# Head copies by engines to the other 64 partitions, and rotations whose partner rows are added by an accumulating DMA

## The chip, the cores and the metric

The kernel runs on one core of one Trainium2 chip. The metric is the device time of one execution in microseconds (us); lower is better. A core has a matrix engine (TensorE, PE in the profile), a vector engine (VectorE, DVE), a scalar engine (ScalarE, ACT), a general engine (GpSimd, POOL) and a sync engine (SyncE, SP). Each runs its own instructions strictly in the order in which they were written, and waits for the others through semaphores. SP and POOL also issue DMA transfers: those of SP go to the queue "hardware_dynamic" of the profile, those of POOL to "software_dynamic", and the same 16 DMA engines work on both.

## The reference

Two layers run over 528 rows (16 learned tokens and 512 inputs) of width 1024. Each layer makes one large projection and splits it into a convolution group and an attention group:

```python
proj = jnp.einsum('bld,de->ble', h, w_in[l])
a, g, zc, q, k, v, za, qi, ki, wi = jnp.split(proj, IN_SPLITS, axis=-1)
y_conv = conformer_conv_branch(a, g, zc, ...)      # GLU, 31-tap causal conv, LayerNorm, SiLU, gate
q = apply_rope(q.reshape(B, Lp, N_HEADS, HEAD_DIM), cos_h, sin_h)
k = apply_rope(k.reshape(B, Lp, N_HEADS, HEAD_DIM), cos_h, sin_h)
qi = apply_rope(qi.reshape(B, Lp, N_IDX_HEADS, IDX_DIM), cos_h, sin_h)
ki = apply_rope(ki, cos, sin)
y_attn = dsa_sparse_attention(q, k, v, qi, ki, wi, topk) * jax.nn.silu(za)
h = layer_norm(DEEPNORM_ALPHA * h + concat(y_conv, y_attn) @ w_out[l], ...)
```

`apply_rope` turns pairs of channels: `x1*cos - x2*sin` and `x2*cos + x1*sin`. The sparse attention first scores all keys with the indexer heads `qi`, `ki`, keeps the 132 best per query, and attends to these alone. There are 8 attention heads and 8 indexer heads of 64 channels.

## The kernel before

Everything is held transposed: channels lie on the 128 partitions and positions along the free axis. A row tile is 128 x 528 and so holds two heads of 64 channels. Columns of a weight are loaded in halves of 128 x 512 (256 KB): SP loads the half into `wraw` (7 buffers), ACT copies it to `whi` (4 buffers, the rounded high part), ACT writes its negative to `wlo` (5 buffers), and POOL issues a DMA that adds `wraw` to `wlo`, so that `wlo` is the low part. A product is then three runs of matmuls, high by high (`hh`, `whi`), low by high (`hl`, `whi`) and high by low (`hh`, `wlo`).

The work is cut into named jobs: `i0`-`i3` make the indexer queries, `kw` the indexer key and its weights, `s12` and `s34` the scores and top-k on DVE, `q`, `k`, `v`, `a` the parts of a pair of heads, `t0`-`t3` the attention of a pair, `u`, `z`, `c01`, `c23`, `cl` the convolution group, `o0`-`o7` and `oa` the output projection, `ln` the closing norm. `ORDER` gives the order in which jobs are recorded. A planner then schedules all recorded operations with a cost for each (`_price`), a delay from each operation to the ones that depend on it (`delay`), and a shift in time for each job (`SHIFT`), and writes the instructions of each engine in the order that it found. All operations are recorded in one place, so nearly every instruction of a trace has the same line, and the tiles tell them apart.

The functions that matter here are three. `rope` rotates a row tile `x`: rows are stored so that partners lie on neighbouring partitions, two DMAs on SP copy odd rows to even rows and back into `rot`, and DVE makes `x*cos`, `rot*sin` and their sum. `heads_q` splits a rotated tile into high and low parts and lays them out so that one tile holds, for one head, the high part in its own 64 partitions and the low part in the other 64: two copies on ACT, a subtraction on DVE into `lq`, and two DMAs on SP to the other partitions. `heads_k` makes tiles that hold a head's high part (`k0`, `k1`) or its low part (`kl`, `km`) in both halves: three copies on ACT, one subtraction on DVE, and four DMAs on SP. `job_kw` copies the indexer key to both halves of `ki` by two DMAs. Per layer there are eight calls of `heads_q` (four of jobs `i`, four of `q`), four of `heads_k`, and thirteen of `rope`.

Of the kernel before, what the change touches and what calls it, by code (L numbers as in the profile page):

```python
# [8 lines left out]
F32 = mybir.dt.float32  # L9
F32R = mybir.dt.float32r  # L10
BF = mybir.dt.bfloat16
AF = mybir.ActivationFunctionType
OP = mybir.AluOpType
# [6 lines left out]
L = SEQ + NM  # L20
DEPTH = 2
NH = 8
HD = 64
# [10 lines left out]
C_KW = 32  # L34
# [10 lines left out]
)  # L45
SHIFT = {
# [21 lines left out]
}  # L68
W1 = NM + P
K_COS = 0  # L70
K_SIN = L
# [13 lines left out]
class Planner:  # L85
# [84 lines left out]

    def delay(self, a, b, true):
        if a.dma:
            far = 650.0 if a.eng == "pool" else 1950.0
            return far + a.tail + (900.0 if b.eng == "sp" else 1067.0 if b.eng == "pe" else 950.0)
        if a.eng == b.eng and (not true or a.eng == "pe"):
            return 0.0
        return self.LAT.get((a.eng, b.eng), 120) + (200.0 if (a.eng, b.eng, a.tail) == ("dve", "act", 1)
                                                    else 0.0)
# [161 lines left out]
def tile_hymba(ctx: ExitStack, tc: tile.TileContext, xt: bass.AP, wi: bass.AP, wv: bass.AP,  # L340
# [3 lines left out]
    pe, act, dve, pool, sync = (pl.engine(e) for e in ("pe", "act", "dve", "pool", "sp"))  # L344
# [28 lines left out]
    def weight(src, eng, kt=KT, into=None, step=KT // 2):  # L373
        W = [], []
        for k in range(0, kt, step):
            r = T(wp, [P, KT // 2, P], F32, name="wraw", tag="wraw", bufs=7)[:, :step, :]
            sync.dma_start(r, src[:, k:k + step, :])
            if into:
                h, o = [t[:, k:k + step, :] if len(t.shape) == 3 else t for t in into]
                if len(h.shape) == 4:  # L380
                    r = r.rearrange("p (r c) n -> p r c n", r=2)
            else:
                h, o = [T(wp, [P, KT // 2, P], F32R, name=n, tag=n, bufs=b)[:, :step, :]
                        for n, b in (("whi", 4), ("wlo", 5))]
            act.activation(h, r, AF.Copy)
            if eng is pool:
                act.activation(o, r, AF.Copy, scale=-1.0)
                pool.dma_start(o.bitcast(F32), r, accum_op=OP.add)
            else:
                eng.tensor_tensor(o, r, h.bitcast(F32), op=OP.subtract)  # L390
            for w, t in zip(W, (h, o)):
                w.extend(t[:, n, :] if len(t.shape) == 3 else t[:, n // 2, n % 2, :] for n in range(step))
        return W
# [22 lines left out]
    cosT = konst[:, K_COS:K_COS + L]  # L416
    sinT = konst[:, K_SIN:K_SIN + L]
# [25 lines left out]
    for l in range(DEPTH):  # L443
# [4 lines left out]
        def spans(lo):  # L448
            return [(lo, L)] if L - lo <= 512 else [(max(a, lo), b) for a, b in HALVES]

        def project(col, lo, evac):
            w = weight(wi[l, col], *(fresh.pop(0)() if fresh else (pool,)))
            for a, b in spans(lo):
                acc = T(ps, [P, 512], F32, name="acc", tag="acc", bufs=3)[:, :b - a]
                product(acc, w, lambda k: HI[:, k, a:b], lambda k: LO[:, k, a:b])
                evac(acc, a, b)

        def row(name, dt=F32):
            tag, n = {"xq": ("x", 2), "xk": ("x", 2), "ki": ("x", 2), "vt": ("x", 2), "rot": ("rot", 2),
                      "lq": ("lq", 2), "sg": ("sg", 1)}.get(name, ("rl", ROWS))  # L460
            return T(sp, [P, L], dt, name=name, tag=tag, bufs=n)

        def copy_to(x, scale=1.0):
            return lambda acc, a, b: act.activation(x[:, a:b], acc, AF.Copy, scale=scale)

        def rope(x, a):
            rot = row("rot")
            for g in range(2):
                sync.dma_start(rot[g::2, a:], x[1 - g::2, a:])
            dve.tensor_mul(x[:, a:], x[:, a:], cosT[:, a:])  # L470
            dve.tensor_mul(rot[:, a:], rot[:, a:], sinT[:, a:])
            dve.tensor_add(x[:, a:], x[:, a:], rot[:, a:])

        def split(x, a, hi, lo):
            act.activation(hi[:, a:], x[:, a:], AF.Copy)
            dve.tensor_tensor(lo[:, a:], x[:, a:], hi[:, a:].bitcast(F32), op=OP.subtract)

        def heads_q(col, a, keep, scale=1.0):
            x = row("xq")
            project(col, a, copy_to(x, scale))  # L480
            rope(x, a)
            s0, s1 = keep("s0"), keep("s1")
            lo = row("lq", F32R)
            split(x, a, s0, lo)
            act.activation(s1[64:, a:], x[64:, a:], AF.Copy)
            sync.dma_start(s1[:64, a:].bitcast(F32), lo[64:, a:].bitcast(F32))
            sync.dma_start(s0[64:, a:].bitcast(F32), lo[:64, a:].bitcast(F32))
            return s0, s1

        def heads_k(col, keep):  # L490
            x = row("xk")
            project(col, 0, copy_to(x))
            rope(x, 0)
            s0, s1, l0, l1 = (keep(n) for n in ("k0", "k1", "kl", "km"))
            split(x, 0, s0, l0)
            act.activation(s1[64:, :], x[64:, :], AF.Copy)
            act.activation(l1[64:, :], l0[64:, :], AF.Copy)
            for one, two in ((s0, s1), (l0, l1)):
                sync.dma_start(two[:64, :].bitcast(F32), two[64:, :].bitcast(F32))
                sync.dma_start(one[64:, :].bitcast(F32), one[:64, :].bitcast(F32))  # L500
            return (s0, s1), (l0, l1)

        def dots(qs, ks, kls, q0, m, a, b):
            out = [T(ps, [P, 512], F32, name="pl", tag="s", bufs=2)[:m, :b - a] for _ in range(2)]
# [7 lines left out]
        kw = T(sp, [P, L], F32, name="kw", tag="s01")  # L512
# [6 lines left out]

        def job_kw():  # L520
            ki = row("ki")
            project(C_KW, 0, copy_to(kw))
            for s in (0, 64):
                sync.dma_start(ki[s:s + 64, :], kw[0:64, :])
            rope(ki, 0)
            split(ki, 0, kih, kil)
            po = turn(ki, P)
            act.activation(kihr, po, AF.Copy)
            dve.tensor_tensor(kilr, po, kihr.bitcast(F32), op=OP.subtract)
# [188 lines left out]
        def keep(j):  # L718
            return lambda name: T(sp, [P, L], F32R, name=name, tag=f"{name}{j % 2}")

        def job_q(j):
            ready[j, "q"] = (heads_q(C_Q + j, qlo, keep(j), -HD ** -0.5),)
# [135 lines left out]
        for i in range(2):  # L858
            pl.job = f"ln{i}/{l}"
            a, b, _ = chunks(i)  # L860
            norm(lambda j: R[j // 4][:, j % 4, :], KT, mean_c[:, 0, :], i, V_PG, pool, i == 1)
            for j in range(KT):
# [4 lines left out]
                else:  # L867
# [6 lines left out]
                    if not last and j % 2:  # L874
                        pool.tensor_tensor(LO[:, j, a:b], r, HI[:, j, a:b].bitcast(F32),
                                           op=OP.subtract)
# [68 lines left out]
```

## Time and profile before

| | us |
|---|---|
| Median of 3 runs | 675.14 (672.87 to 675.35) |
| The profiled execution | 671.79 |
| Its span, first to last instruction | 669.8 |
| PE busy / DVE busy | 639.0 / 524.0 |
| ACT busy / POOL busy | 463.8 / 191.9 |
| Mean granted TensorE clock | 0.989 of full speed |

Matmuls are pipelined, so PE counts as busy from the start of one to the modelled end of the next, and a busy PE may still be spaced more widely than it could be. A wait in the profile is the idle time just before an instruction, put down to the semaphore that came last.

### The profile page before, as it was taken

Reading aid. Unit: us, or ns where it says so; the run is one execution under the profiler, and the core shown is the slowest. Engines: PE = TensorE matmul, PEld = TensorE weight load, DVE = VectorE, ACT = ScalarE, POOL = GpSimd, SP = SyncE. Lnnn points to the kernel's source line nnn. Section 1 sums busy time; section 2 is a strip of 40 time slices with the busy share of each in tenths; the row PEclk is TensorE's granted clock in tenths of the full one; section 3 lists DMA queues with packets and bytes.
Section 4 is the critical chain, followed back from the end, with each engine's and each line's share of the span. In section 5 each row is a group of like instructions: output and inputs, shape, how many; then the busy total and the mean of one; then the engine's idle time right before and its main releaser. Section 6 shows DMA issues by size and latency. Waiting matters only on the chain.

```text
span 669.8 us, 13204 instructions
## 1 busy us (share of the span) xinstructions
PE 639.0 (95%) x4602; PEld 598.1 (89%) x4602; DVE 524.0 (78%) x1279; ACT 463.8 (69%) x1056; POOL 191.9 (29%) x236
## 2 busy tenths in 40 slices
PE   8999999999999998899999999999999999989993
PEld 7989999999999987899898999888999889967992
DVE  5686999999899947444563999999999999483356
ACT  7554865865756979596676665667549887895536
POOL 0423213223211322444543232223231121233262
PEclk8999999999999999899999999999999999999997
DMA  8899849748855586998315985887886783279503
GB/s 299 203 263 219 237 95 236 168 98 197 198 131 130 127 224 170 200 212 199 75 68 139 225 212 131 191 212 173 189 186 163 166 188 90 87 177 238 82 1 125
DMA packets 67570, 112.60 MB, mean 168 GB/s; under 512 B 7600, under 2 KB 21168, under 8 KB 67376
## 3 DMA queue, kind: packets, MB, share of 16 engines
q0 software_dynamic: 25088, 41.95, 37.5%
q1 hardware_dynamic: 42416, 69.81, 33.2%
q8 instruction: 36, 0.59, 0.3%
q14 instruction: 30, 0.25, 0.1%
HBM read 50.46 MB, written 4.26 MB: 82 GB/s over the span
## 4 chain that ended last, share of the span: by engine, by line
PE 56%; issue 15%; DMA 9%; DVE 6%; ACT 5%; POOL 2%; SPq 0%; POOLq 0%; ACTq 0%; DVEq 0%
PE acc L297 28%; PE acco L297 11%; DMA wlo<-wraw 5%; PE o L297 5%; PE pl L297 3%; PE pp L297 3%; PE pq L297 2%; POOL wlo L297 2%; DVE r L297 2%; DVE sc L297 1%; DMA s<-lq 1%; PE pm L297 1%; DMA kl<-kl 1%; DMA qi<-lq 1%; DMA rot<-xq 1%
## 5 line engine op out<-in xcount | busy, mean ns | idle before, releaser
L297 POOL DMA_DIRECT2D wlo<-wraw x140 | 124.0, 939 | 350.7 <-ACT wlo L297 214.1
L297 DVE SCALAR_TENSOR_TENSOR conv<-u,vec,conv 128x528 f32<-128x528 f32 (+1 forms) x240 | 176.4, 755 | 1.8
L297 PE MATMUL acc<-hh,whi 128*128 128x272 f32 (+3 forms) x872 | 154.0, 308 | 5.0 <-ACT hh L297 2.5
L297 PE MATMUL acc<-hl,whi 128*128 128x272 f32 (+3 forms) x872 | 148.1, 303 | 0.0
L297 PE MATMUL acc<-hh,wlo 128*128 128x272 f32 (+3 forms) x872 | 144.5, 304 | 3.8 <-DMA wlo<-wraw 3.5
L297 PEld LDWEIGHTS acc<-hh,whi 128*128 128x128 f32 x872 | 125.1, 190 | 11.7 <-ACT hh L297 3.9
L297 PEld LDWEIGHTS acc<-hh,wlo 128*128 128x128 f32 x872 | 123.8, 190 | 10.7 <-DMA wlo<-wraw 6.2
L297 ACT ACTIVATE whi<-wraw 128x512 fp32r<-128x512 f32 (+1 forms) x148 | 86.9, 614 | 66.3 <-PE acc L297 51.1
L297 PEld LDWEIGHTS acc<-hl,whi 128*128 128x128 f32 x872 | 124.6, 190 | 3.9 <-issue 0.2
L297 ACT ACTIVATE wlo<-wraw 128x512 fp32r<-128x512 f32 x140 | 85.5, 623 | 6.9 <-PE acc L297 4.8
L297 DVE SCALAR_TENSOR_TENSOR r<-r,acco 128x256 f32<-128x256 f32 (+2 forms) x56 | 25.8, 462 | 47.4 <-PE acco L297 47.3
L297 DVE MAX8 m<-sc 128x8 f32<-128x400 f32 (+3 forms) x106 | 55.9, 551 | 0.0
L297 DVE MATCH_REPLACE8 sc<-m,sc 128x400 f32<-128x400 f32 (+3 forms) x98 | 53.6, 549 | 0.0
L297 ACT ACTIVATE p<-p,ast 128x400 f32<-128x400 f32 (+4 forms) x72 | 40.6, 568 | 5.0 <-DVE ast L297 4.7
L297 PE MATMUL o<-v,pt 128*128 128x64 f32 x320 | 43.0, 265 | 0.5 <-ACT pt L297 0.4
L297 PEld LDWEIGHTS o<-v,pt 128*128 128x128 f32 x320 | 41.5, 192 | 1.7 <-ACT pt L297 1.1
L297 ACT ACTIVATE rl<-pl 128x272 f32<-128x272 f32 (+3 forms) x80 | 29.5, 391 | 14.8 <-PE pl L297 12.1
L297 DVE CUSTOM_DVE_ANT_0 p<-pl,bmask 128x272 f32<-128x272 f32 (+3 forms) x80 | 33.0, 433 | 7.7 <-PE pl L297 6.2
L297 ACT ACTIVATE pt<-pp 128x128 f32<-128x128 f32 (+3 forms) x64 | 26.9, 433 | 11.5 <-PE pp L297 10.7
L297 ACT ACT_TABLE_LOAD x26 | 33.4, 1283 | 1.5 <-PEq L936 0.7
L297 DVE SCALAR_TENSOR_TENSOR sc<-rl,ws,sc 12x144 f32<-12x144 f32 (+3 forms) x56 | 29.9, 555 | 0.6 <-ACT rl L297 0.3
L297 PE MATMUL pp<-konst,p 128*128 128x128 f32 x160 | 30.2, 289 | 0.0
(167 smaller groups left out, 1067.5 us busy)
## 6 DMA issues: line engine op xcount, KB each, us to landing
wlo<-wraw POOLq DMA_DIRECT2D x140, 256.0 KB, 4.9
wraw<-wi SPq DMA_DIRECT2D x128, 256.0 KB, 3.8
wraw<-wo SPq DMA_DIRECT2D x32, 256.0 KB, 4.1
hl<-wraw POOLq DMA_DIRECT2D x16, 256.0 KB, 5.2
rot<-xk SPq DMA_DIRECT2D x16, 132.0 KB, 2.7
k<-k SPq DMA_DIRECT2D x16, 132.0 KB, 3.1
r<-xt SPq DMA_DIRECT2D x2, 1056.0 KB, 8.9
r<-spill SPq DMA_DIRECT2D x2, 1024.0 KB, 6.2
```

Of the source, the lines that this page charges most:

```text
L297: self.plan.record(self.e, fn, lambda: real(*a, **k), reads, writes, *_price(self.e, fn, named, reads, writes))
```

## The change

In `rope` the products come first: `rot = x*sin` with the signs of the table turned round, then `x = x*cos`, and then two DMAs issued by POOL add the rows of `rot` to their partner rows of `x` in flight. The DVE addition is gone, and so are the two DMAs on SP. In `heads_q` the subtraction writes straight to the other 64 partitions, as two instructions of 64 partitions each, and the two DMAs on SP are gone. In `heads_k` six copies on ACT and two subtractions on DVE fill both halves, without the four DMAs. `job_kw` fills `ki` from the accumulator by two more copies on ACT for each part of the row. The planner's delay behind a DMA of POOL is 1800 ns in place of 650 ns, and `SHIFT` has other numbers throughout; `ORDER` is as it was.

```diff
 SHIFT = {
-    "a0/1": 301146, "a1/0": -624491, "a1/1": -132089, "a2/0": 1188874, "a2/1": -413625,
+    "a0/0": 128058, "a0/1": -2790, "a1/0": -360296, "a1/1": -41383, "a2/0": -466571,
...
-            far = 650.0 if a.eng == "pool" else 1950.0
+            far = 1800.0 if a.eng == "pool" else 1950.0
...
         def rope(x, a):
             rot = row("rot")
-            for g in range(2):
-                sync.dma_start(rot[g::2, a:], x[1 - g::2, a:])
+            dve.tensor_mul(rot[:, a:], x[:, a:], sinT[:, a:])
             dve.tensor_mul(x[:, a:], x[:, a:], cosT[:, a:])
-            dve.tensor_mul(rot[:, a:], rot[:, a:], sinT[:, a:])
-            dve.tensor_add(x[:, a:], x[:, a:], rot[:, a:])
+            for g in range(2):
+                pool.dma_start(x[g::2, a:], rot[1 - g::2, a:], accum_op=OP.add)
...
-            s0, s1 = keep("s0"), keep("s1")
-            lo = row("lq", F32R)
-            split(x, a, s0, lo)
-            act.activation(s1[64:, a:], x[64:, a:], AF.Copy)
-            sync.dma_start(s1[:64, a:].bitcast(F32), lo[64:, a:].bitcast(F32))
-            sync.dma_start(s0[64:, a:].bitcast(F32), lo[:64, a:].bitcast(F32))
-            return s0, s1
+            ss = keep("s0"), keep("s1")
+            for g, t in enumerate(ss):
+                own, other = x[64 * g:64 * g + 64, a:], slice(64 - 64 * g, 128 - 64 * g)
+                hi = t[64 * g:64 * g + 64, a:]
+                act.activation(hi, own, AF.Copy)
+                dve.tensor_tensor(t[other, a:], own, hi.bitcast(F32), op=OP.subtract)
+            return ss
...
-            s0, s1, l0, l1 = (keep(n) for n in ("k0", "k1", "kl", "km"))
-            split(x, 0, s0, l0)
-            act.activation(s1[64:, :], x[64:, :], AF.Copy)
-            act.activation(l1[64:, :], l0[64:, :], AF.Copy)
-            for one, two in ((s0, s1), (l0, l1)):
-                sync.dma_start(two[:64, :].bitcast(F32), two[64:, :].bitcast(F32))
-                sync.dma_start(one[64:, :].bitcast(F32), one[:64, :].bitcast(F32))
-            return (s0, s1), (l0, l1)
+            hs, ls = [[keep(n) for n in ns] for ns in (("k0", "k1"), ("kl", "km"))]
+            for g, (h, t) in enumerate(zip(hs, ls)):
+                own, other = slice(64 * g, 64 * g + 64), slice(64 - 64 * g, 128 - 64 * g)
+                act.activation(h[own, :], x[own, :], AF.Copy)
+                dve.tensor_tensor(t[own, :], x[own, :], h[own, :].bitcast(F32), op=OP.subtract)
+                act.activation(h[other, :], x[own, :], AF.Copy)
+                act.activation(t[other, :], t[own, :].bitcast(F32), AF.Copy)
+            return hs, ls
...
-            project(C_KW, 0, copy_to(kw))
-            for s in (0, 64):
-                sync.dma_start(ki[s:s + 64, :], kw[0:64, :])
+
+            def evac(acc, a, b):
+                act.activation(kw[:, a:b], acc, AF.Copy)
+                for g in (0, 64):
+                    act.activation(ki[g:g + 64, a:b], acc[:64], AF.Copy)
+            project(C_KW, 0, evac)
...
-    cst[:, K_SIN:K_SIN + L] = np.tile(np.stack([-sn, sn], axis=1).reshape(HD, L), (2, 1))
+    cst[:, K_SIN:K_SIN + L] = np.tile(np.stack([sn, -sn], axis=1).reshape(HD, L), (2, 1))
```

Three places show how the instructions stand, all towards the end of layer 1, where the last pair of heads (`k3`, `q3`) is made beside the output projection. First SP, before: the DMAs of the rotations, the eight copies of `k3` and `q3`, and the loads of output weights (`wraw<-wo`) between and behind them.

```order
L297 DMA rot_1543<-xk_1534 64x528 x2
L297 DMA wraw_1641<-wo 128x512
L297 DMA rot_1561<-xq_1553 64x512 x2
L297 DMA r1_1624<-spill 128x4x512
L297 DMA k1_1545<-k1_1545 64x528
L297 DMA k0_1544<-k0_1544 64x528
L297 DMA km_1547<-km_1547 64x528
L297 DMA kl_1546<-kl_1546 64x528
L297 DMA wraw_1642<-wo 128x512
L297 DMA s1_1563<-lq_1564 64x512
L297 DMA s0_1562<-lq_1564 64x512
L297 DMA wraw_1644<-wo 128x512
```

The same place of SP with the change:

```order
L299 DMA wraw_1613<-wo 128x512
L299 DMA wraw_1604<-wo 128x512
L299 DMA wraw_1617<-wo 128x512
L299 DMA wraw_1621<-wo 128x512
L299 DMA r1_1608<-spill 128x4x512
L299 DMA wraw_1625<-wo 128x512
L299 DMA wraw_1626<-wo 128x512
```

SP has only loads of weights and of the residual left there. Next POOL at this place, before: the DMAs that make the low parts of the output weights stand next to each other.

```order
L297 DMA wlo_1618<-wraw_1616 128x512
L297 DMA wlo_1627<-wraw_1625 128x512
L297 DMA wlo_1631<-wraw_1629 128x512
L297 DMA wlo_1635<-wraw_1633 128x512
L297 DMA wlo_1622<-wraw_1620 128x512
L297 DMA hl_71<-wraw_1641 128x2x256
```

POOL there with the change (`xk_1519` is the row tile of `k3`, `xq_1538` that of `q3`):

```order
L299 DMA wlo_1551<-wraw_1549 128x512
L299 DMA xk_1519<-rot_1528 64x528 x2
L299 DMA wlo_1602<-wraw_1600 128x512
L299 DMA wlo_1611<-wraw_1609 128x512
L299 DMA wlo_1615<-wraw_1613 128x512
L299 DMA xq_1538<-rot_1546 64x512 x2
L299 DMA wlo_1619<-wraw_1617 128x512
L299 DMA wlo_1606<-wraw_1604 128x512
```

The two pairs of rotation DMAs now stand between low parts of weights, which wait behind them. Last ACT at the same place, before, with the three copies for `k3` (`k0`, `k1`, `km`) and the first two for `q3`:

```order
L297 ACTIVATE wlo_1635<-wraw_1633 128x512
L297 ACTIVATE k0_1544<-xk_1534 128x528
L297 ACTIVATE k1_1545<-xk_1534 64x528
L297 ACTIVATE whi_1617<-wraw_1616 128x512
L297 ACTIVATE wlo_1622<-wraw_1620 128x512
L297 ACTIVATE km_1547<-kl_1546 64x528
L297 ACTIVATE yah_928<-y_1491 128x512
L297 ACTIVATE s0_1562<-xq_1553 128x512
L297 ACTIVATE s1_1563<-xq_1553 64x512
```

ACT there with the change:

```order
L299 ACTIVATE whi_1601<-wraw_1600 128x512
L299 ACTIVATE k0_1529<-xk_1519 64x528
L299 ACTIVATE k1_1530<-xk_1519 64x528
L299 ACTIVATE k0_1529<-xk_1519 64x528
L299 ACTIVATE k1_1530<-xk_1519 64x528
L299 ACTIVATE kl_1531<-kl_1531 64x528
L299 ACTIVATE km_1532<-km_1532 64x528
L299 ACTIVATE wlo_1606<-wraw_1604 128x512
```

Six copies for `k3` follow each other, and the next low part of a weight stands behind them.

## Rows read from the trace of the kernel before

**Rows 1.** The page, part 1: busy us, share of the span, instructions.

```profile
PE 639.0 (95%) x4602; PEld 598.1 (89%) x4602; DVE 524.0 (78%) x1279; ACT 463.8 (69%) x1056; POOL 191.9 (29%) x236
```

**Rows 2.** Windows of 20 us: busy us (instructions) by engine, clock, DMA share, GB/s.

```profile
260.00:280.00 20.00, 15.87 (x114) 15.30 (x114) 9.19 (x23) 14.67 (x35) 8.07 (x8) 0.91 0.92 212
...
480.00:500.00 20.00, 20.00 (x146) 18.84 (x145) 19.97 (x55) 9.56 (x19) 7.04 (x8) 1.00 0.83 184
...
580.00:600.00 20.00, 18.56 (x102) 15.27 (x101) 16.16 (x40) 19.61 (x44) 7.49 (x11) 1.00 0.49 125
600.00:620.00 20.00, 17.83 (x92) 14.61 (x92) 7.50 (x21) 12.79 (x31) 6.16 (x7) 1.00 1.01 232
```

**Rows 3.** Waits of PE: who waited for whom, total us, times, longest us.

```profile
PE acco L297 <- DMA wlo<-wraw: 5.0, 2, 4.1
PE acc L297 <- DMA wlo<-wraw: 3.5, 5, 1.2
...
PE pl L297 <- DMA s<-lq: 1.3, 1, 1.3
```

**Rows 4.** Timeline of PE, four places: start us, us, instruction, count, idle before.

```profile
95.85 1.11 PE L297 MATMUL acc<-hh,whi 128*128 128x256 f32 x8
96.80 1.11 PE L297 MATMUL acc<-hl,whi 128*128 128x256 f32 x8
...
270.11 1.23 PE L297 MATMUL acco<-ych,wlo 128*128 128x256 f32 x4 [4.13 <-DMA wlo<-wraw]
...
597.77 1.09 PE L297 MATMUL acco<-ych,whi 128*128 128x512 f32 x4
598.70 1.09 PE L297 MATMUL acco<-ycl,whi 128*128 128x512 f32 x4
...
612.16 0.34 PE L297 MATMUL pl<-k,s 128*128 128x144 f32 x1 [1.26 <-DMA s<-lq]
```

**Rows 5.** Timeline of SP and ACT, 590 to 612 us.

```profile
591.16 0.57 ACT L297 ACTIVATE xq<-acc 128x512 f32<-128x512 f32 x1
...
597.85 1.79 SPq L297 DMA_DIRECT2D k<-k  x2
...
605.47 3.23 SPq L297 DMA_DIRECT2D s<-lq  x2
...
610.09 0.63 ACT L297 ACTIVATE hl<-wraw 128x512 fp32r<-128x512 f32 x1 [5.31 <-DMA wraw<-wo]
```

**Rows 6.** Tiles xq and km: duration ns min/median/max, first to last start us.

```profile
L297 ACT ACTIVATE xq<-acc x20: 362/488/599, 30.9 to 591.2; 128x396 f32<-128x396 f32 x8, 128x272 f32<-128x272 f32 x4, 128x256 f32<-128x256 f32 x4, 128x512 f32<-128x512 f32 x4
L297 DVE TENSOR_TENSOR xq<-xq,rot x16: 552/626/707, 41.7 to 598.4; 128x396 f32<-128x396 f32 x8, 128x528 f32<-128x528 f32 x4, 128x512 f32<-128x512 f32 x4
L297 ACT ACTIVATE s<-xq x16: 615/630/647, 111.4 to 600.9; 128x528 fp32r<-128x528 f32 x4, 64x528 fp32r<-64x528 f32 x4, 128x512 fp32r<-128x512 f32 x4, 64x512 fp32r<-64x512 f32 x4
...
L297 ACT ACTIVATE km<-kl x8: 640/641/643, 104.6 to 599.0; 64x528 fp32r<-64x528 f32 x8
```

**Rows 7.** Tile wlo: issues on POOL, and times from issue to landing.

```profile
L297 POOL DMA_DIRECT2D wlo<-wraw x140: 856/869/1702, 17.2 to 604.5; - x140
...
DMA to landing us min/median/max: 3.3/4.9/9.4
```

**Rows 8.** DMA queues (packets, MB, share of 16 engines) and issues (KB each, us).

```profile
q0 software_dynamic: 25088, 41.95, 37.5%
q1 hardware_dynamic: 42416, 69.81, 33.2%
...
k<-k SPq DMA_DIRECT2D x16, 132.0 KB, 3.1
...
rot<-xq SPq DMA_DIRECT2D x16, 99.0 KB, 4.6
```

**Rows 9.** Timeline of DVE, two neighbouring instructions.

```profile
92.39 0.44 DVE L297 MAX8 m<-sc 128x8 f32<-128x272 f32 x1
92.74 0.75 DVE L297 SCALAR_TENSOR_TENSOR conv<-u,vec,conv 128x528 f32<-128x528 f32 x1
```

More of the change, by code (lines that the diff above doesn't have):

```diff
@@ L467, in rope @@
             rot = row("rot")
+            dve.tensor_mul(rot[:, a:], x[:, a:], sinT[:, a:])
+            dve.tensor_mul(x[:, a:], x[:, a:], cosT[:, a:])
             for g in range(2):
-                sync.dma_start(rot[g::2, a:], x[1 - g::2, a:])
-            dve.tensor_mul(x[:, a:], x[:, a:], cosT[:, a:])
-            dve.tensor_mul(rot[:, a:], rot[:, a:], sinT[:, a:])
-            dve.tensor_add(x[:, a:], x[:, a:], rot[:, a:])
+                pool.dma_start(x[g::2, a:], rot[1 - g::2, a:], accum_op=OP.add)
         def split(x, a, hi, lo):
```

42 rows, old and new, of the table SHIFT are left out of this document.

## The prediction

> **What bounds the kernel now.** I read the page first. PE is busy 639.0 us of the span of 669.8, and DVE, ACT and POOL have 524.0, 463.8 and 191.9 [rows 1]. So PE sets the time unless another engine holds it up. The windows say where that could be: in the middle of a layer PE and DVE are full together (20.00 and 19.97 of 20 us), at the start of the output projection PE falls to 15.87, 18.56 and 17.83, once with a granted clock of 0.91, once with ACT full (19.61), once with the DMA engines full (1.01) [rows 2]. In full stretches matmuls are spaced as closely as anywhere: eight of 256 columns take 0.95 us, 0.119 us each, and four of 512 columns 0.93 us, 0.23 each [rows 4]. The change removes and adds no work for PE. What it can win or lose is PE's idle time, 669.8 - 639.0 = 30.8 us, part of it at the two ends. The list of PE's waits names two kinds that the change touches: for the low parts of weights, 5.0 us in two and 3.5 us in five waits, and for the head copies, 1.3 us in one [rows 3]. The timeline puts the longest of the first kind, 4.13 us, at 270 us, and the last at 612 us [rows 4].
>
> **The change part by part.** *Head copies by DMA go.* The wait at 612.16 is for `s<-lq`. The row tile had left the accumulator at 591.16, 21 us earlier, and the copy was issued at 605.47, behind the four copies of `k3` and a load in SP's queue [rows 5]. The new way: evacuation 0.57, two products on DVE at 0.63, a first DMA issue at 0.87, the second from issue to landing 4.9 (9.4 at most), two copies at 0.63, a subtraction at 0.63: 9.5 us, 14.0 with the slowest landing [rows 5 to 7]. I count in the new order 58 matmuls of 512 columns between the last product of that tile and its first use, 58 x 0.23 = 13.3 us [rows 4]: enough but for the slowest landing. Value -1.3, bounds 0 and -1.3. The 5.31 us that ACT waits at 610.09 for output weights, which stood behind those copies on SP, also go [rows 5]; but no wait of PE for them is on the list, so they count as 0.
>
> *The planner's delay.* It now counts 1.15 us more behind each weight DMA of POOL. The measured time from issue to landing is 4.9 us in the median and 9.4 at most [rows 7]. If uses are planned 1.15 us later after issue and the order is otherwise as good, the five waits of at most 1.2 us and the short one of the pair vanish: 3.5 + (5.0 - 4.1) = 4.4 us [rows 3]. The long one of 4.13 us came with a drop to the lower of the two clock levels (0.91 over 20 us is 1.8 us lost) [rows 2, 4]; I leave it standing. The bounds are 0, since a new order has new waits of its own, and -4.4 - 4.1 - 1.8 = -10.3. I take -4.4, for the new numbers in `SHIFT` say nothing against it.
>
> *DVE.* Each of 26 rotations loses an addition (0.63), each of 24 head jobs gains a second subtraction of the same length: 2 x 0.63 less, which is 0. The cover is none in full windows, where DVE matters; so the other bound is the second rival's.
>
> *ACT.* Each `k` job has six copies of 0.64 for three: 8 x 3 x 0.64 = 15.4 us, and each `kw` four more evacuations of about 0.4, 3.2 us in all [rows 6]. ACT has 206 us idle, so most is hidden. It is not where ACT is full: the last `k` job (its `km` copy is at 599.0) lies in the window with 19.61 of 20 [rows 2, 6]. There 1.9 us more pass before the low part behind the copies, and PE waits in that window already. Value +1.5; bounds 0 and 3.8, if layer 0 has the same.
>
> *POOL.* 52 issues at 0.87 are 45 us more on an engine idle for 478 [rows 1, 7]. They wait for DVE, and low parts of weights wait behind them, in POOL's order. For each rotation I count the matmuls from its last product to the first use of a low part queued behind it. The nearest of the 26 is `i3` in layer 1, with 83 matmuls of about 256 columns, 83 x 0.119 = 9.9 us; scaled by columns in the same way the others have 11.7 us or more. Needed are evacuation 0.49, two products 1.25, two issues 1.74 and 4.9 for the weight itself, 8.4 us [rows 4, 6, 7]. So this is covered by the matmuls in between, with 1.5 us to spare at the nearest and 3.3 at the next: 0. Without the cover see the first rival.
>
> *A new short distance.* `q2` in layer 1 is used 83 matmuls after its last product, 43 of them of 256 or 272 columns and the rest short: between 5.1 us (43 x 0.119) and 9.9. The chain above needs 9.5 [rows 4 to 7]. Bounds 0 and 9.5 - 5.1 = 4.4, taken near the low one since a short matmul still takes most of the spacing of a long one: +0.7.
>
> *DMA engines.* 120 transfers of 99 to 132 KB leave the queue of SP, some 14.2 MB, and 52 such, 6.2 MB, come to POOL's. By the queues' shares SP's cost 0.332 x 669.8 / 69.81 = 3.2 us of all 16 engines per MB and accumulating ones 0.375 x 669.8 / 41.95 = 6.0 [rows 8]. That is 45 us less and 37 more, a gain of 8 us spread over the span: 1.2%, or 0.25 us in each 20 us with full DMA engines. Two such stretches: -0.5, bounds 0 and -1.
>
> *Sum.* -1.3 - 4.4 + 1.5 + 0.7 - 0.5 = -4.0 us, from 671.8 to 667.8 for the profiled execution. That execution lies 2.0 above its span and 3.3 below the median of the runs shown, 675.14; from the median the sum gives **671.1**.
>
> **The rivals.** *Slower: the low parts wait for DVE.* A rotation's DMA cannot be issued before DVE has made both products, and DVE runs its instructions in order. Where DVE is full [rows 2], every tap of the convolution ahead of the products is 0.75 [rows 9]. It decides from the point where DVE comes to the products more than 1.5 us (`i3`) or 3.3 us (the others) later than PE's progress calls for: five taps. Ten of the 26 pairs late by 1.2 us beyond that are +12 us: 683. For it: before, nothing on POOL waited for the rotations. Against it: a wait of DVE's products of two or more taps beyond plan has to happen often.
>
> *No change: the half subtractions don't overlap.* Neighbouring DVE instructions overlap: one starts at 92.74 while the one before ends at 92.39 + 0.44 = 92.83, 0.09 us [rows 9]. The new ones read from and write to partitions 0 or 64 by turns. If every change of the starting partition costs that overlap, a `q` or `i` job has three such places (both subtractions and the next instruction) and a `k` job two, 16 x 3 + 8 x 2 = 64, 64 x 0.09 = 5.8 us of DVE. Where DVE and PE are full together about two thirds of it would reach the end, which leaves 671.1 + 3.9 = 675. The Trainium skill (VectorE: DVE Perf Modes, section "Two Vector instructions with no wait between them") states it: an instruction that starts in another group of 32 partitions than the last input or output is held until all earlier ones have finished. No DVE instruction of the kernel before starts elsewhere than at partition 0, so no row shows it; if the rule holds here the forecast moves to the 675 above.
>
> *More: the long stall goes too.* With loads no longer behind head copies the stall at 270 us and its clock may go as well, 4.1 + 1.8 us beyond the sum: 665.
>
> **How the numbers follow.** Forecast 0.46, slower 0.20, no change 0.16, more 0.18. Half a per cent (3.4 us) is about what a measurement of this kernel can tell from no change. The forecast's own range is 667 to 675; about 0.30 of its 0.46 lies below 671.8, 0.14 between, 0.02 above 678.5. So faster 0.30 + 0.18 = 0.48; same 0.14 + 0.14 = 0.28; slower 0.20 + 0.02 + 0.02 = 0.24. The range reaches to 661 (the delay's bound of -10.3, with the other savings and the costs about even) and to 683 (the first rival).
>
> **What the profile would show.** Waits for `s<-lq` must be gone, SP's list of waits must hold none for ACT's or DVE's head tiles, and PE's waits for `wlo` should be below 5 us in sum. POOL should be busy some 45 us more, ACT some 18, DVE within 3 unless the half subtractions lose their overlap. The forecast is wrong if POOL's waits name DVE's `rot` or `x` before weight DMAs and PE's waits for `wlo` grow, if the accumulating DMAs land later than 4.9 us in the median, or if ACT is held up behind the copies that wait for them.

## The result, and the profile after

The changed kernel took **656.8 us** in the median (655.56 to 657.88, 4 runs) beside 675.25 of the kernel before (672.87 to 675.52, 4 runs): a ratio of **0.9734**, interval 0.9706 to 0.9762, or 18.4 us less. The forecast of 671.1 had the sign right and a quarter of the size; 656.8 lies below the 661 where its range ends.

Part 1 of the page after, which answers to [rows 1]:

```profile
PE 634.6 (97%) x4602; PEld 597.5 (91%) x4602; DVE 523.7 (80%) x1277; ACT 473.7 (72%) x1085; POOL 237.2 (36%) x288
```

The span is 654.8, 15.0 less than that of before, whose profiled execution (671.79) lay 3.5 below that median; PE's idle time fell from 30.8 to 20.2 us; another 4.4 us went out of PE's busy time, which a wider spacing of matmuls and a lower clock had held (0.91 before and 1.00 after in the windows 0 to 20 and 260 to 280). DVE is as it was, ACT has 9.9 us more, POOL 45.3. The windows that answer to [rows 2]:

```profile
260.00:280.00 20.00, 20.00 (x166) 19.48 (x166) 8.49 (x32) 17.96 (x45) 10.04 (x10) 1.00 1.11 235
480.00:500.00 20.00, 20.00 (x140) 18.48 (x139) 19.90 (x54) 14.68 (x34) 6.99 (x8) 1.00 0.64 145
580.00:600.00 20.00, 19.93 (x99) 16.27 (x98) 10.33 (x25) 17.73 (x39) 9.82 (x11) 1.00 1.10 251
600.00:620.00 20.00, 20.00 (x150) 18.92 (x149) 7.55 (x22) 11.06 (x27) 6.66 (x6) 1.00 0.62 105
```

All three gaps at the output projections are filled, the granted clock of the first is 1.00 for 0.91, and that with the DMA engines at 1.11 and 1.10 in the windows from 260 and from 580, where they had 0.92 and 0.49 before. The waits of PE, in the columns of [rows 3]:

```profile
PE acc L299 <- ACT hh L299: 3.1, 4, 1.4
PE rb L299 <- POOL st L299: 1.3, 1, 1.3
PE acc L299 <- ACT xq L299: 1.0, 2, 0.7
...
PE acc L299 <- DMA wlo<-wraw: 0.5, 1, 0.5
```

The waits for low parts went from 8.5 us in seven to 0.5 in one, and none is left for `s<-lq`. The next list reads this better. It has the weight loads (PEld), which stand ahead of the matmuls: a late low part holds the load first, and part of that shows as wider spacing of matmuls and not as idle PE. Before:

```profile
PEld acc L297 <- DMA wlo<-wraw: 6.2, 10, 1.4
PEld acco L297 <- DMA wlo<-wraw: 5.7, 2, 4.3
```

After:

```profile
PEld acc L299 <- DMA wlo<-wraw: 0.7, 1, 0.7
...
PEld acco L299 <- DMA wlo<-wraw: 0.3, 1, 0.3
```

That is 11.9 us in 12 waits against 1.0 in two. The DMAs themselves are not faster. The tile `wlo`, as in [rows 7], has the same issues on POOL, and the page's list of DMA issues has 4.8 us to landing in the median:

```profile
L299 POOL DMA_DIRECT2D wlo<-wraw x140: 856/862/1896, 17.2 to 592.2; - x140
...
wlo<-wraw POOLq DMA_DIRECT2D x140, 256.0 KB, 4.8
```

So the low parts land as late after issue as before, but are read later. The queues and the new DMAs, as in [rows 8], and the tile `rot`:

```profile
q0 software_dynamic: 29248, 48.41, 43.9%
q1 hardware_dynamic: 32816, 54.73, 25.2%
...
L299 POOL DMA_DIRECT2D xq<-rot x32: 835/1174/1533, 31.3 to 582.7; - x32
...
  DVE xk L299: 16.8, 6
  DVE xq L299: 15.1, 7
...
DMA to landing us min/median/max: 2.6/4.5/8.2
```

The record of an accumulating issue has 1.17 us in the median, but that is not what it costs POOL. The two of a rotation overlap, the second starting before the record of the first ends, so that a pair takes 1.71 us, as here on POOL's timeline:

```profile
577.02 1.71 POOL L299 DMA_DIRECT2D xk<-rot  x2 [1.10 <-DVE conv L299]
```

The 45.3 us that POOL has more are 0.87 for each of the 52 issues, as in the forecast. POOL does wait for DVE ahead of them, 31.9 us in 13 waits, as the rival "slower" says, but the weight loads wait no more than the 1.0 us above for low parts. On SP the long waits for head tiles are gone (21.4 us for `k` of ACT and 15.7 for `lq` of DVE before); rows that name ACT's head tiles have 0.9 us at most, and SP issues no DMA of these any more. What SP waits for now is room for the next weights:

```profile
SPq L299 <- DMA wlo<-wraw: 380.8, 119, 19.5
```

Last DVE, where two half subtractions of a head follow each other (`x2`), to be read beside [rows 9]:

```profile
108.13 0.76 DVE L299 SCALAR_TENSOR_TENSOR conv<-u,vec,conv 128x528 f32<-128x528 f32 x1
108.81 1.30 DVE L299 SCALAR_TENSOR_TENSOR sc<-rl,ws,sc 128x528 f32<-128x528 f32 x2
110.14 1.42 DVE L299 TENSOR_TENSOR s<-xq,s 64x528 fp32r<-64x528 f32 x2
111.57 0.77 DVE L299 SCALAR_TENSOR_TENSOR conv<-u,vec,conv 128x528 f32<-128x528 f32 x1
```

The second row starts 0.08 us before the first ends (108.89); the half subtractions start 0.03 after theirs (110.11), and the instruction behind them 0.01 after their end (111.56). Over the whole trace, neighbouring DVE instructions that follow within 0.2 us overlap by 0.078 us in the median (1093 pairs); of the 74 pairs with a half subtraction, 63 don't overlap but stand 0.031 apart in the median. The other 11 overlap by 0.05 to 0.09: they are those into and out of a subtraction that writes `kl`, except where the next one writes `km`. `kl` is read from and written to partition 0, like the instructions around it, so it is the change of the starting partition and not the 64 partitions that goes with the lost overlap.

### The profile page after: what moved, and what is told of

Read it like the earlier page. It is cut to its first block, busy times and chain, and to the rows that moved or that the text cites. A ratio compares the mean times of both kernels' runs of the same rounds, so it can differ in the third digit from the quotient of the medians.

```text
span 654.8 us, 13099 instructions
## 1 busy us (share of the span) xinstructions
PE 634.6 (97%) x4602; PEld 597.5 (91%) x4602; DVE 523.7 (80%) x1277; ACT 473.7 (72%) x1085; POOL 237.2 (36%) x288
## 3 DMA queue, kind: packets, MB, share of 16 engines
q1 hardware_dynamic: 32816, 54.73, 25.2%
## 4 chain that ended last, share of the span: by engine, by line
PE 73%; DVE 13%; ACT 8%; issue 2%; DMA 1%; POOL 1%; SPq 0%; ACTq 0%; DVEq 0%; POOLq 0%
PE acc L299 39%; PE acco L299 14%; PE o L299 6%; PE pl L299 6%; DVE conv L299 5%; PE pp L299 3%; DVE sc L299 3%; PE pq L299 2%; DVE m L299 2%; ACT r L299 1%; DVE r L299 1%; PE pm L299 1%; ACT hh L299 1%; ACT wlo L299 1%; DMA wlo<-wraw 1%
## 5 line engine op out<-in xcount | busy, mean ns | idle before, releaser
L299 POOL DMA_DIRECT2D wlo<-wraw x140 | 129.6, 976 | 267.8 <-ACT wlo L299 128.0
L299 DVE MAX8 m<-sc 128x8 f32<-128x528 f32 (+3 forms) x106 | 55.7, 551 | 0.0
L299 DVE MATCH_REPLACE8 sc<-m,sc 128x528 f32<-128x528 f32 (+3 forms) x98 | 53.5, 549 | 0.0
L299 ACT ACTIVATE p<-p,ast 128x144 f32<-128x144 f32 (+4 forms) x72 | 40.8, 571 | 2.7 <-DVE ast L299 2.5
L299 ACT ACTIVATE rl<-pl 128x272 f32<-128x272 f32 (+3 forms) x80 | 28.9, 388 | 14.8 <-PE pl L299 7.5
L299 POOL DMA_DIRECT2D xq<-rot x32 | 28.2, 1045 | 28.4 <-DVE xq L299 15.1
```

What stands on the lines that cost most here:

```text
L299: self.plan.record(self.e, fn, lambda: real(*a, **k), reads, writes, *_price(self.e, fn, named, reads, writes))
```

## The experiments

Two theories were to be told apart. **Operations**: the new rotations and copies make the chains shorter, and that is the gain. **Planner**: the gain is the delay of 1800 ns, with a table `SHIFT` that is fitted to the program with that delay. The order of the whole program depends on the table, so no edit of the code can be tried with "the same order", and the edits are tried with three kinds of tables. In each batch the kernel before ran beside the others (674.0 to 676.0).

**Empty tables.** Old and new code, each with a delay of 650 and 1800:

```diff
-SHIFT = {
-    "a0/1": 301146, "a1/0": -624491, "a1/1": -132089, "a2/0": 1188874, "a2/1": -413625,
...
-}
+SHIFT = {}
...
-            far = 650.0 if a.eng == "pool" else 1950.0
+            far = 1800.0 if a.eng == "pool" else 1950.0
```

Old code, 650: 

> The kernel before with an empty table of shifts, delay 650. Both theories: slower than 675, by 10 to 60 us, since the order is the planner's own. It is the base of the next three. Theory 1 (the gain is in the code: head copies and rotations without DMAs of SP) and theory 2 (the gain is in the numbers: the delay of 1800 and the new shifts) part in the next three.

Old code, 1800: 

> The kernel before with an empty table of shifts, delay 1800. Theory 2 (delay): 5 us or more faster than the same with 650, PE's waits for low parts of weights at most half. Theory 1 (code): within 3 us of it.

New code, 1800: 

> The changed kernel with an empty table of shifts, delay 1800. Theory 1 (code): at least 8 us faster than the kernel before with an empty table and the same delay. Theory 2: within 4 us of it.

New code, 650: 

> The changed kernel with an empty table of shifts, delay 650. Theory 1 (code): within 3 us of the same with 1800 and at least 8 us faster than the kernel before with an empty table and 650. Theory 2 (delay): 5 us or more slower than the same with 1800.

Measured: old 683.06 (8 us above the kernel before, where 10 to 60 were expected) and 681.41, new 678.49 and 668.08 (650 and 1800; each within 0.35% by its interval). The delay gives 1.7 with the old code and 10.4 with the new; the code gives 4.6 at 650 and 13.3 at 1800. Taken alone these four speak for the operations, in the main, though neither theory has all four: the code's 4.6 at 650 is below the 8 that the operations should give, and the delay's 1.7 below the 5 of the planner.

**Tables of the other kernel, and delay alone.** The old code with its own table and the delay of 1800; the same with the new table; the new code with the old table; the new code and table with the delay of 650. The edits are those of the code in the section on the change, the two tables as they stand in the two kernels, and for the first of the four the delay alone:

```diff
-            far = 650.0 if a.eng == "pool" else 1950.0
+            far = 1800.0 if a.eng == "pool" else 1950.0
```

Delay alone on the kernel before: 

> The kernel before with its own table of shifts and the delay of 1800. Table theory (a table fits one program with one delay, and the difference of 675 and 657 is mostly the two tables): slower than 675.2 by 5 us or more. Delay theory (the forecast's largest term): 4 us faster than 675.2, 671.

Delay of 1800 and new table, old code: 

> The kernel before with the new table of shifts and the delay of 1800. Code theory: at least 8 us slower than the changed kernel's 656.8, so 665 or more, as the empty table showed 13. Table theory: within 5 us of 656.8.

New code, old table, 1800: 

> The changed kernel with the old table of shifts, delay 1800. Code theory: at least 8 us faster than the kernel before with the same table and delay. Table theory: no faster than that one, 670 to 685.

The changed kernel with a delay of 650: 

> The changed kernel with its own table of shifts and the delay of 650. If the planner must know when the accumulating DMAs land: 8 us or more slower than 656.8, as with the empty table (10). If the delay mattered only there by chance: within 4 us.

Measured: 680.87, 676.85, 682.52 and 676.46. The delay alone makes the kernel before slower by 5.3 us beside the 675.62 of its batch (ratio 1.0072, 1.0049 to 1.0096), and taking it from the changed kernel costs 19.7 (656.80 in the first batch). With the same old table and 1800 the new code lies 1.7 above the old, which their intervals don't tell apart. The new table does nothing for the old code: 676.85, where the theory of the table expected it within 5 us of 656.8. A table is thus worth something only with the code and the delay that it was fitted for, and comparisons across such tables say little of the operations.

**Tables fitted alike.** So each code and delay got a table of its own: a random search over `SHIFT`, from the empty table, of the same length for all four, that kept what made the planner's own plan shorter. The edit against the kernels with empty tables is the table alone, here that of the old code at 1800:

```diff
-SHIFT = {}
+SHIFT = {
...
+}
```

Old code, 650: 

> The old code with the old delay of 650 and numbers in SHIFT chosen anew for it, by a random search of one length for all four kernels of this batch, from the empty table, judged by the length that the kernel's own planner gives its plan. If the changed operations are what makes the changed kernel fast (theory code), no table helps the old ones much: 670 to 675 here and in the next kernel. If what counts is a table fitted to a planner that knows the late landing (theory delay), a table fitted with 650 keeps little of what it plans: 670 to 675 here too, but much less in the next. If any fitted table will do, 660 or so here.

Old code, 1800: 

> The old code, delay 1800, and numbers in SHIFT chosen anew for this pair. Theory code: 670 to 675, as the kernel before. Theory delay: the old operations give nearly the time of the changed kernel, 657 to 663, since with empty tables old and new code lay 13 us apart at 1800 but with unfitted tables of other kinds only 4 apart in the mean.

New code, 1800: 

> The new code, delay 1800, and numbers in SHIFT chosen anew by the same search: both theories have 655 to 661, about the changed kernel's 656.8, since it differs from it in the table alone. If it stays at the 668 of the empty table, a fitted table is worth less than the changed kernel lets one think, and that kernel's numbers are a lucky draw.

New code, 650: 

> The new code with the old delay of 650 and numbers in SHIFT chosen anew for it. Theory code: 657 to 662, since the operations are the new ones. Theory delay: 666 to 673, since the table is fitted to landings that come later than planned, and uses of low parts stand too close behind their DMAs again, which should show as waits of PE for the low parts.

| | 650 | 1800 |
|---|---|---|
| old code | 669.86 (0.9921 to 0.9961) | 660.79 (0.9777 to 0.9839) |
| new code | 668.32 (0.9879 to 0.9936) | 660.90 (0.9783 to 0.9855) |

In brackets the interval of the ratio to the kernel before. The columns differ by 9.1 and 7.4 us, the rows by 1.5 and nothing. The theory of the operations wanted 670 to 675 for the old code at 1800, and 657 to 662 for the new code at 650; it falls at both. The chain that ended last (page, part 4: by engine, then by line) shows what the delay does. Old code, 650:

```profile
PE 47%; issue 24%; DMA 11%; ACT 8%; DVE 5%; POOL 4%; SPq 1%; POOLq 0%; ACTq 0%; DVEq 0%
PE acc L295 23%; PE acco L295 11%; DMA wlo<-wraw 6%; PE o L295 4%; POOL wlo L295 4%; PE pl L295 3%; DMA wraw<-wo 2%; PE pp L295 2%; PE pq L295 2%; DMA wraw<-wi 2%; DVE conv L295 1%; DVE r L295 1%; ACT wlo L295 1%; ACT conv L295 1%; ACT L295 1%
```

and its waits of weight loads, where low parts stand first:

```profile
PEld acc L295 <- DMA wlo<-wraw: 7.0, 11, 1.6
...
PEld acco L295 <- DMA wlo<-wraw: 1.1, 2, 0.8
```

The long stall of the kernel before at 270 us is already gone here, with the old code, the old head copies and the old delay; the window of 260 to 280 in this kernel:

```profile
260.00:280.00 20.00, 19.41 (x155) 18.64 (x154) 11.14 (x34) 16.46 (x43) 8.28 (x8) 1.00 1.09 252
```

**Second tables, and half of the change.** What was open then: whether the two halves of the new operations cancel, and how much one fitted table differs from another. Only the new rotations (with the old head copies), only the new head copies and `kw` job (with the old rotations), and the new and the old code with a second table from another start of the search, all at 1800 (the search for the copies was shorter). The edits against the old code with an empty table, cut to their core:

```diff
         def rope(x, a):
...
-            dve.tensor_add(x[:, a:], x[:, a:], rot[:, a:])
+            for g in range(2):
+                pool.dma_start(x[g::2, a:], rot[1 - g::2, a:], accum_op=OP.add)
```

Rotations alone: 

> Only the new rotations (two products, accumulating DMAs of POOL), the old head copies, delay 1800, a table fitted by the same search. If the operations don't matter: 659 to 663, as old and new code with fitted tables (660.8 and 660.9). If the halves win and lose the same: one of this kernel and the next lies 3 us or more below 660.8, the other as far above; the rotations would be the loser by POOL's order (low parts wait for DVE), so 664 or more here.

```diff
         def heads_q(col, a, keep, scale=1.0):
...
-            sync.dma_start(s1[:64, a:].bitcast(F32), lo[64:, a:].bitcast(F32))
+                dve.tensor_tensor(t[other, a:], own, hi.bitcast(F32), op=OP.subtract)
```

Copies alone: 

> Only the new head copies and kw job, the old rotations by two DMAs on SP, delay 1800, a table fitted by the same search. If the operations don't matter: 659 to 663. If the halves win and lose the same: 657 or less here, since the copies leave SP's queue at the price of ACT, which is idle a third of the time.

New code, second table: 

> The new code at 1800 with a second fitted table, found from another start of the random search. If one table differs from another by as much as the changed kernel differs from the first (4 us): anywhere from 656 to 665. If equally fitted tables agree: 659.5 to 662.5, and the changed kernel's table is better fitted than these.

Old code, second table: 

> The old code at 1800 with a second fitted table. The same: 659.5 to 662.5 if equally fitted tables agree, 656 to 665 if a table is worth 4 us either way. Above 665 would mean that the 660.8 of the first table was a lucky draw and the operations do count.

Measured: rotations alone **659.87**, copies alone **660.96**, new code **662.71** (0.9809 to 0.9847), old code **657.72** (0.9709 to 0.9813). No half wins or loses, so nothing cancels. Neither second table fell into the 659.5 to 662.5 that equal tables would have: two of one code differ by 1.8 (new) and 3.1 (old) in the medians, which their intervals don't tell apart (the old code's second has runs from 654.64 to 663.12). The old operations with the second table are not told apart from the changed kernel, 657.7 beside 656.8. Their chain, to be read beside the one at 650 above:

```profile
PE 61%; DVE 18%; ACT 9%; issue 6%; DMA 4%; POOL 1%; SPq 1%; POOLq 0%; ACTq 0%; DVEq 0%
PE acc L290 33%; PE acco L290 11%; DVE sc L290 7%; DVE m L290 5%; PE o L290 5%; PE pl L290 5%; PE pp L290 2%; PE pq L290 2%; DVE conv L290 2%; DMA wraw<-wi 1%; DVE r L290 1%; DMA s<-lq 1%; ACT L290 1%; ACT whi L290 1%; DVE xk L290 1%
```

and their only wait of a weight load for a low part:

```profile
PEld acc L290 <- DMA wlo<-wraw: 0.9, 1, 0.9
```

The chain ran 11% through DMAs and 24% through "issue" at 650, with the low parts third in the list of lines; at 1800 it has 4% and 6%, and `wlo` is not in the list. The other fitted kernels lie between the two (8% and 13% in the new code at 650, 3 to 8% and 3 to 6% at 1800), but for the old code's first table at 1800, whose chain the page can follow over a quarter of the span only. The halves also settle DVE's share of the change. Rotations alone, then copies alone, from part 1 of their pages:

```profile
PE 636.4 (96%) x4602; PEld 598.3 (91%) x4602; DVE 508.3 (77%) x1253; ACT 468.1 (71%) x1060; POOL 238.4 (36%) x288
```

```profile
PE 633.5 (96%) x4602; PEld 596.2 (91%) x4602; DVE 538.8 (82%) x1303; ACT 478.0 (73%) x1087; POOL 193.6 (29%) x236
```

Beside the 524.0 of [rows 1] the rotations save DVE 15.7 us and the copies cost it 14.8. Neither shows in the time.

For each of the 140 low parts the trace has its landing and the first matmul that reads it. Those read within 0.3 us of landing, and the weight loads' waits for them, in the kernels with fitted tables (the kernel before and the changed one, with their own, among them):

| delay | kernels, us | read within 0.3 us | PEld waits for `wlo`, us |
|---|---|---|---|
| 650 | before 675.25, old 669.86, new 668.32 | 16, 16, 15 | 11.9, 8.1, 6.9 |
| 1800 | old 660.79 and 657.72, new 660.90 and 662.71, rotations 659.87, copies 660.96, changed 656.80 | 6, 1, 6, 10, 5, 6, 5 | none listed, 0.9, 2.5, 1.2, 0.8, 2.1, 1.0 |

The fitted tables of 650 pack reads onto low parts that have only just landed. It is the order that moves away from the landing, not the landing from the order: the median from issue to landing is 4.8 to 5.1 us in the three of 650 and 4.8 to 5.4 in the seven of 1800. The changed kernel with its own table and the delay alone set back to 650 has 21 such reads for 5, and 9.3 us of waits for 1.0. Few such reads are not enough by themselves: the kernel before with its own table and 1800 has 5 and takes 680.87. With empty tables the counts are low at both delays (7 and 6 at 650), so there the time lies elsewhere: such orders are long for other reasons.

The granted clock differs as well. Its mean over a run, averaged over the runs of each kernel, is 0.987 for the kernel before, 0.988 for the two kernels fitted at 650, 0.991 for the six at 1800 and 0.993 for the changed kernel. What the clock takes away is then 9.1, 8.4, 6.1 and 4.7 us of the span, if PE had been busy all the time. That is an estimate and an upper one, since the clock is low in the last microseconds too, where PE has no work left. What makes it fall in one order and not in another was not tested.

**A longer delay.** If 1800 leaves something, 2600 should give it:

```diff
-            far = 1800.0 if a.eng == "pool" else 1950.0
+            far = 2600.0 if a.eng == "pool" else 1950.0
```

New code, table fitted from the empty one: 

> The new code with a delay of 2600 and a table fitted by the same search from the empty one. If 1800 takes all that there is to take: 659 to 663, as the fitted new code at 1800 (660.9 and 662.7). If late landings still cost there: 655 to 658, with fewer low parts read within 0.3 us of their landing than the 5 or 6 at 1800. A longer delay could also cost, as buffers of low parts are held longer in the plan: 664 or more.

The changed kernel, its table fitted further: 

> The changed kernel with a delay of 2600, its own table fitted further for that delay. If 1800 is enough: 656 to 660, the changed kernel's time or a little more. If late landings still cost: 652 to 655, below both kernels.

Measured: **668.14** and **663.34** (ratios 0.9900 and 0.9843). The first is in the range of a delay that costs, the second in neither of its two. Only 2 low parts are read within 0.3 us in each, and weight loads wait 1.1 and 1.0 us for them, so hardly anything was left to win there. In the first the order now has waits of another kind:

```profile
PE acc L290 <- ACT hh L290: 4.5, 3, 2.3
PE pm L290 <- POOL z L290: 4.4, 1, 4.4
```

`z` holds sums for a mean that PE makes; the wait stands at 563.9 us, and the window of 560 to 580 has a granted clock of 0.91. In the new code at 1800, with its first table, the same two rows have 1.3 and 1.2 us, but other rows are longer there; what makes up the 6 us by which this kernel is longer was not followed to the end. In the second it is the clock that stands out. Its two windows with a low clock ahead of the close:

```profile
0.00:20.00 20.00, 16.58 (x76) 14.78 (x77) 9.22 (x30) 12.37 (x29) 1.49 (x8) 0.83 0.83 277
...
340.00:360.00 20.00, 17.37 (x107) 16.75 (x106) 6.94 (x16) 17.52 (x40) 8.35 (x12) 0.83 0.43 107
```

The same windows of the changed kernel:

```profile
0.00:20.00 20.00, 17.72 (x88) 15.73 (x89) 9.83 (x31) 12.71 (x29) 1.48 (x8) 1.00 0.88 288
...
340.00:360.00 20.00, 18.45 (x130) 17.81 (x131) 8.24 (x18) 13.45 (x30) 9.13 (x11) 1.00 0.68 169
```

Up to 2 x 0.17 x 20 = 6.8 us lie in these two, if PE had been busy throughout, beside a difference of 6.4 between the spans (661.2 and 654.8). All four runs have a mean clock of 0.981 to 0.984, where the changed kernel has 0.989 to 0.995. So 2600 is no gain, but that the delay itself costs is not shown.

## Why the prediction was wrong

*The planner's delay* is the step that failed, in two ways. **Its size**: the forecast took -4.4, the five short waits and the short one of the pair. With tables fitted alike it measured -8.6: 669.1 in the mean of two kernels at 650 (669.86, 668.32), 660.5 in the mean of six at 1800. That is within the bound of -10.3. The price was read from the wrong list: PE's matmuls waited 8.5 us for low parts, its weight loads 11.9. In the table above the loads' waits fall from 7.5 (mean of the two fitted at 650) to 1.3 (mean of the six at 1800), 6.2 of the 8.6. The clock may hold up to 2.3 more (8.4 less 6.1, the estimate above); that part is not shown.

**The sentence "the new numbers in `SHIFT` say nothing against it"** set the table at 0. It holds the rest: from 675.25 to the 669.1 of tables fitted here at 650 is 6.1 us, and from 660.5 to the 656.8 of the changed kernel's own table another 3.7. The three parts, 6.1 + 8.6 + 3.7, are the 18.4. The long stall of 4.1 us, which the forecast left standing, belongs to the table: in the old code fitted at 650 the loads of the output projection (`acco`) wait 0.8 us at most for a low part, for 4.3 before, and the window from 260 has a clock of 1.00. So the rival **more** was right that the stall and its clock go, and wrong about the reason, for that kernel still has its head copies on SP. And the delay is worth its 8.6 only together with a table fitted to it: without one it was +5.3 (the old table), -1.7 and -10.4 (empty tables).

*Head copies by DMA go*, *ACT*, *new short distance* and *DMA engines* sum to +0.4 in the forecast. The operations as a whole measured between -1.5 (at 650) and +2.6 (at 1800, means of two tables each, 661.8 and 659.3), and the two tables of one code differ by as much. So about 0 was right, but no run shows the +1.5, the +0.7 or the -0.5 by itself, and that they add up to it is in part luck. Two sizes were off: 15.1 MB left SP's queue and not 14.2, and the two queues together have 21 us less of all 16 engines (57 less on SP's, 36 more on POOL's), not 8. The wait for `s<-lq` did go, -1.3; in the old code with its first table at 1800 it is 0.3 us, and in the one with its second table 2.6, so a table moves it too. ACT got 9.9 us and not 18.6: three table loads of 1.28 us fewer, by its order, are 3.8 of the difference (copies alone, with one fewer, have 14.2 more than before); the rest was not followed. No wait of PE for an `s` tile is on the list, so `q2` in layer 1 costs nothing.

*DVE*, 0: right within 3 us, 523.7 for 524.0, by a saving of 15.7 and a cost of 14.8; with tables fitted alike at 1800 it is 3 us more (524.9 and 525.1 for 521.4 and 521.9).

*POOL*, 0: right, with 45.3 us of issues for the forecast 45. The rival **slower** has its sign, POOL's waits for `xk` and `xq` from DVE, but rotations alone took 659.9, no more than the old code, and its weight loads wait 0.8 us for low parts: these were issued early enough.

The rival **no change** has its mechanism. The half subtractions lose their overlap at 63 places (64 in the forecast) by 0.078 + 0.031 = 0.11 us, 6.9 us of DVE for the forecast 5.8. The Trainium skill (VectorE: DVE Perf Modes, section "Two Vector instructions with no wait between them") has an instruction that starts in another group of 32 partitions held until all earlier ones have finished; the trace agrees, with 63 pairs 0.031 us apart and the 11 at partition 0 overlapping. What failed is its price at the end: copies alone, which hold all 48 half subtractions, took 661.0, beside 660.8 and 657.7 of the old code. That DVE is full for part of a layer only, and that the planner places the rest around it, would explain this; it was not tested.

What stays open: why the changed kernel's table is some 4 to 6 us better than the two fitted here for the same code. Up to 2.0 us of it may be the clock (6.7 in the mean of those two less 4.7, estimated as above). A longer search may do it, or the new operations may leave a search more room; the old code's second table lies 0.9 us from it, which speaks for the search, but none of equal length was made for the old code.

## What to carry to other kernels

Where a planner orders the program, a change of code, its delays and its fitted table are one thing: fit the table anew for the code without the change before the change gets the credit. A delay that is too short does not show in a plan but as reads that stand right behind landings, so count these in the trace, and look at the waits of weight loads and not of matmuls alone. A longer delay is not the safer choice by itself: both orders made with 2600 took longer than those with 1800. And before a difference of a few us between two orders is put down to their waits, compare their granted clocks.

## What the runs showed of the hardware

An accumulating DMA on every second partition (64 rows, 99 to 132 KB) takes POOL 0.87 us to issue, as one of 128 rows and 256 KB does (0.86); its record shows 1.17 in the median only because the records of a pair overlap (1.71 us for two). It lands 4.5 us after issue in the median, hardly sooner than the 4.8 of the larger one. The DMA engines' share of POOL's queue rose by 0.439 x 654.8 - 0.375 x 669.8 = 36 us for 6.46 MB, 5.6 us of all 16 engines per MB; SP's costs 0.252 x 654.8 / 54.73 = 3.0.

DVE instructions that follow each other at partition 0 overlap by 0.078 us in the median; where the starting partition changes between 0 and 64 they stand 0.031 apart, at 63 places of the changed kernel.
